# A softmax with relative position bias: the first loads are cut into pieces and spread over two DMA queues

## The chip, the cores and the metric

The kernel runs on one core of a Trainium2 chip. The core has engines that each run their own list of instructions: VectorE (DVE), ScalarE (ACT), GpSimd (POOL), SyncE (SP) and TensorE (PE, unused here). Data moves between the chip's memory (HBM) and the on-chip buffer (SBUF, 128 partitions) by DMA transfers, which an engine only issues; 16 DMA engines carry them out. The metric is the time of one execution in microseconds (us), the median of the runs; lower is better.

## The reference

Inputs are `logits` of shape 2 x 8 x 2112 x 2112 (float32) and a table `rel_bias` of 8 heads x 33 entries. For every head h, query i and key j the kernel adds a bias that depends on i - j alone, clipped to 16 on both sides, and takes the softmax over j:

```python
rel_clipped = np.clip(pos[:, None] - pos[None, :], -16, 16) + 16
logits = logits + rel_bias[:, rel_clipped][None]
exp = np.exp(logits - logits.max(axis=-1, keepdims=True))
return exp / exp.sum(axis=-1, keepdims=True)
```

Every element is read once and written once: 285.48 MB in and 285.48 MB out.

## The kernel before

**Tiling.** Partition p holds the rows of one head and one of 16 row regions, 132 rows of 2,112 elements for each of the two batches. A *chunk* is 6 such rows in every partition: 128 partitions x 12,672 elements, 6,336 KB, held by one of four buffers X0 to X3. A *window* is the four chunks m = 0 to 3 (two batches, two groups of six rows); 11 windows k = 0 to 10 make the whole, so there are 44 chunks. One partition's share of a chunk is one contiguous run of 50,688 B in HBM; in the texts below this run, which moves as one DMA packet, is called a **strip** (it holds six softmax rows).

**The order of work.** Everything is written by hand with semaphores; there is no scheduler.

- SP (lines 83 to 102): issues the four loads of window 0 at once (`load(0, m)`, line 99 calls line 91), then in a loop waits until the store of buffer m has landed (`take(nc.sync, st[m], 16)`) and issues the next window's load into that buffer. All loads of `logits` are on SP's queue (q1 in the profile).
- DVE: first a prologue (lines 120 to 169) that builds a table F of biases; then, per window, one copy of a part of it (`window`, line 172), and per chunk `add` (line 186, six instructions: add the bias, keep the negated row maximum), a reciprocal (line 210) and four of the six rescalings (line 213). `add(m)` begins with `take(v, ld[m], 16)`, that is: it waits until the chunk's load has landed.
- ACT: per chunk six exponentials (line 197), two rescalings (line 218), then it waits for all six rescaled rows and issues the store (line 95). All stores are on ACT's queue (q10), as is one small load of `rel_bias` in the prologue (line 122).

A transfer adds 1 to its semaphore for each DMA engine that is done with its share, by a packet of 4 B behind the share's data, called a **mark** below. 16 marks mean that the transfer has landed. One chunk's transfer is 128 strips and 16 marks: 8 strips and one mark for each DMA engine.

The waits in `take` (line 88) consume the count; the profile names line 88 where an engine was released by such a wait. The code of `add`, `window`, `load` and `store` and what calls them follows.

Of the kernel before, what the change touches and what calls it, by code (L numbers as in the profile page):

```python
# [15 lines left out]
def kernel(  # L16
# [6 lines left out]
    nc = tc.nc  # L23
    P = 128
    B, H, S, S2 = logits.shape
# [3 lines left out]
    RP = H * S // P  # L29
# [4 lines left out]
    NBUF = 4  # L34
    R = 6
    M = NBUF // B
    G = M * R
# [6 lines left out]
    X = [io.tile([P, R * S], FP32, tag=f"X{b}", name=f"X{b}") for b in range(NBUF)]  # L44
# [25 lines left out]
    def rows(t, k, m):  # L70
        return bass.AP(
            tensor=t.tensor, offset=t.offset + (m // M) * (H * S * S) + (m % M) * R * S + k * (G * S), ap=[[RP * S, P], [1, R * S]],
        )

    with tc.tile_critical(no_gpsimd_drain=True):  # L75
        ld = [nc.alloc_semaphore(f"ld{b}") for b in range(NBUF)]
        st = [nc.alloc_semaphore(f"st{b}") for b in range(NBUF)]
# [2 lines left out]
        scaled = nc.alloc_semaphore("scaled")  # L80
        inv = nc.alloc_semaphore("inv")
        rb = nc.alloc_semaphore("rb")
        zero = nc.alloc_semaphore("zero")
        idx = nc.alloc_semaphore("idx")
        dve = nc.alloc_semaphore("dve")

        def take(eng, sem, n):
            eng.wait_ge(sem, n).then_inc(sem, -n)  # L88

        def load(k, m):  # L90
            nc.sync.dma_start(out=X[m][:, :], in_=rows(logits, k, m)).then_inc(ld[m], 16)

        def store(k, m):
            take(nc.scalar, scaled, R)
            nc.scalar.dma_start(out=rows(out, k, m), in_=X[m][:, :]).then_inc(st[m], 16)

        for m in range(NBUF):
            load(0, m)
        with nc.Fori(0, K - 1, 1, engines=[ENG.SP]) as k:
            for m in range(NBUF):  # L100
                take(nc.sync, st[m], 16)
# [11 lines left out]
        def settle():  # L113
# [9 lines left out]
            out=bass.AP(tensor=F2.tensor, offset=F2.offset, ap=[[Q * step, P // Q], [1, H * W]]),  # L123
            in_=bass.AP(tensor=rel_bias.tensor, offset=rel_bias.offset, ap=[[0, P // Q], [1, H * W]]),
        ).then_inc(rb, 16)
        nc.gpsimd.iota(pid[:, :], pattern=[[0, 2]], base=0, channel_multiplier=1).then_inc(idx, 1)
        nc.gpsimd.iota(
            num, pattern=[[1, NB + 1]], base=0, channel_multiplier=0,
# [52 lines left out]

        def add(m):
            take(v, ld[m], 16)
            for i in range(R):
                x = G - 1 - (m % M) * R - i
                v.tensor_tensor_reduce(  # L186
                    out=row(m, i), in0=row(m, i), in1=F2[:, x : x + S],
                    scale=-1.0, scalar=BIG, op0=ALU.add, op1=ALU.min, accum_out=col(nmax, m, i),
                ).then_inc(added, 1)
# [25 lines left out]
        def scale_rest(m):  # L215
            scales_begin(nc.scalar, m)
            for i in range(DV, R):
                nc.scalar.activation(  # L218
                    out=row(m, i), in_=row(m, i), func=ACTF.Copy, scale=col(rec, m, i),
                ).then_inc(scaled, 1)  # L220

        with nc.Fori(0, K, 1, engines=[ENG.DVE]) as k:  # L222
            window(k)
            for m in range(NBUF):
                add(m)
                scale(m)
# [36 lines left out]
```

## Time and profile before

| what | value |
|---|---|
| time, median of 3 runs | 1325.94 us (1325.74 to 1336.57) |
| profiled execution, from its first to its last instruction (span) | 1323.8 us |
| DVE busy | 866.2 us, 65% of the span |
| ACT busy | 757.2 us, 57% |
| DMA | 570.98 MB, mean 431 GB/s |
| queue q1 (loads): packets, share of 16 DMA engines' span | 6336, 50.0% |
| queue q10 (stores and the bias table) | 6344, 49.8% |

The page gives no other time for the profiled execution than its span, which lies 2.1 us below the median of the runs.

How to read it: the page's busy shares of DVE and ACT are averages over the span. The DMA row cuts the span in 40 slices and gives the mean busy share of the 16 DMA engines in tenths; GB/s is what they moved in a slice. In a table of short stretches, a DMA packet counts where it begins, with its whole duration, so that a share can pass 1.00; the bytes divided by 50,688 then tell how many strips began there. A timeline row is start, duration, engine, line, operation, what it writes and reads, and in brackets how long the engine sat idle before it and what released it. An engine name with a q (SPq, ACTq, DVEq) is that engine's sequencer, which runs waits, branches and DMA issues.

### The profile page before, as it was taken

Reading aid. Unit: us, or ns where it says so; the run is one execution under the profiler, and the core shown is the slowest. Engines: PE = TensorE matmul, PEld = TensorE weight load, DVE = VectorE, ACT = ScalarE, POOL = GpSimd, SP = SyncE. Lnnn points to the kernel's source line nnn. Section 1 sums busy time; section 2 is a strip of 40 time slices with the busy share of each in tenths; the row PEclk is TensorE's granted clock in tenths of the full one; section 3 lists DMA queues with packets and bytes.
Section 4 is the critical chain, followed back from the end, with each engine's and each line's share of the span. In section 5 each row is a group of like instructions: output and inputs, shape, how many; then the busy total and the mean of one; then the engine's idle time right before and its main releaser. Section 6 shows DMA issues by size and latency. Waiting matters only on the chain. (4 is left out here: it accounts for less than half of the span.)

```text
span 1323.8 us, 2109 instructions
## 1 busy us (share of the span) xinstructions
DVE 866.2 (65%) x781; ACT 757.2 (57%) x627; POOL 0.4 (0%) x6
## 2 busy tenths in 40 slices
DVE  6886666566766675576667666556766576566662
ACT  3776655556666555555656555555666565555663
POOL 0000000000000000000000000000000000000000
DMA  9999999999999999999999999999999999999998
GB/s 417 417 423 435 441 435 423 441 438 421 440 441 427 430 441 435 424 440 438 424 437 440 437 423 440 440 421 438 441 432 426 441 437 423 440 440 423 437 441 369
DMA packets 12682, 570.98 MB, mean 431 GB/s; under 512 B 1412, under 2 KB 1416, under 8 KB 1416
## 3 DMA queue, kind: packets, MB, share of 16 engines
q1 hardware_dynamic: 6336, 285.48, 50.0%
q10 hardware_dynamic: 6344, 285.48, 49.8%
q14 instruction: 2, 0.02, 0.0%
HBM read 285.48 MB, written 285.47 MB: 431 GB/s over the span
## 5 line engine op out<-in xcount | busy, mean ns | idle before, releaser
L197 ACT ACTIVATE X<-X,nmax 128x2112 f32<-128x2112 f32 x264 | 542.6, 2055 | 505.1 <-DVE nmax L186 472.4
L186 DVE CUSTOM_DVE_ANT_0 X<-X,F 128x2112 f32<-128x2112 f32 x264 | 605.2, 2354 | 319.1 <-DVEq L88 319.1
L213 DVE TENSOR_SCALAR X<-X,rec 128x2112 f32<-128x2112 f32 x176 | 220.3, 1315 | 2.8
L218 ACT ACTIVATE X<-X,rec 128x2112 f32<-128x2112 f32 x88 | 176.1, 2048 | 17.2 <-DVE rec L210 12.2
L210 DVE RECIPROCAL rec<-tot 128x6 f32<-128x6 f32 x44 | 8.4, 191 | 106.2 <-DVEq L88 106.2
L197 ACT ACTIVATION_READ_ACCUMULATOR X<-X,nmax 128x1 f32 x264 | 49.2, 186 | 0.0
L197 ACT ACT_TABLE_LOAD x11 | 14.1, 1283 | 22.6 <-ACTq L88 19.9
L172 DVE COPY F<-F 128x2123 f32 x11 | 26.0, 2361 | 0.5 <-DVEq L88 0.5
L186 DVE DVE_READ_ACCUMULATOR2_ANT nmax<- 128x1 f32 x264 | 21.6, 82 | 0.0
L144 DVE LOAD_MASK_SELECT F<-F x1 | 0.0, 14 | 6.2 <-DMA F<-in_rel_bias_dram 6.2
L164 DVE COPY F<-own 128x1485 f32<-128x1485 f32 x1 | 1.7, 1698 | 0.0
L120 DVE MEMSET F<- 128x264 f32 x1 | 0.3, 278 | 1.1 <-SPq L75 1.1
L142 DVE TENSOR_SCALAR Z<-rec,Z 128x16 f32<-128x16 f32 (+2 forms) x5 | 0.8, 233 | 0.1
L163 DVE TENSOR_TENSOR F<-F,own 128x528 f32<-128x528 f32 x1 | 0.7, 717 | 0.1
L160 DVE TENSOR_TENSOR F<-Z,own 128x528 f32<-128x528 f32 x1 | 0.7, 705 | 0.0
L150 DVE TENSOR_REDUCE own<-F 128x33 f32<-128x264 f32 x1 | 0.6, 609 | 0.1
L147 DVE TENSOR_TENSOR F<-F,Z 128x264 f32<-128x264 f32 x1 | 0.4, 429 | 0.1
L144 DVE STREAM_SHUFFLE F<-F 128x264 f32<-128x264 f32 x1 | 0.4, 442 | 0.0
L158 DVE SCALAR_TENSOR_TENSOR own<-Z,own 128x16 f32<-128x16 f32 x1 | 0.2, 235 | 0.2 <-DVEq L88 0.2
L155 DVE TENSOR_SCALAR own<-Z,own 128x16 f32<-128x16 f32 x1 | 0.2, 235 | 0.2 <-DVEq L88 0.2
L166 DVE COPY F<-own 128x115 f32<-128x115 f32 x1 | 0.3, 271 | 0.0
L168 DVE COPY F<-own 128x115 f32<-128x115 f32 x1 | 0.3, 271 | 0.0
(11 smaller groups left out, 1.6 us busy)
## 6 DMA issues: line engine op xcount, KB each, us to landing
X<-in_logits_dram SPq DMA_DIRECT2D x44, 6336.0 KB, 38.4
out_dram<-X ACTq DMA_DIRECT2D x44, 6336.0 KB, 59.0
F<-in_rel_bias_dram ACTq DMA_DIRECT2D x1, 4.1 KB
```

The source lines that it names most:

```text
L142: then(v.tensor_scalar(out=o, in0=num[:, 0:n], scalar1=s, scalar2=None, op0=op))
L144: then(v.stream_shuffle(out=T, in_=T, mask=[0] * Q))
L150: then(v.tensor_reduce(out=rbK, in_=view(F2, H * W, [[1, W], [W, H]]), axis=mybir.AxisListType.X, op=ALU.add))
L160: then(v.tensor_tensor(out=bands, in0=view(eq, 0, [[1, NB], [0, W]]), in1=view(rbK, W - 1, [[0, NB], [-1, W]]), op=ALU.mult))
L163: then(v.tensor_tensor(out=bands, in0=bands, in1=view(rest, 0, [[1, NB], [0, W]]), op=ALU.add))
L164: then(v.tensor_copy(out=view(F, C0 + W, [[RP, NB - 1], [1, RP - W]]), in_=view(reg, 1, [[1, NB - 1], [0, RP - W]])))
L172: then(v.tensor_copy(out=F2[:, 0:SW], in_=F[:, bass.ds(RP - G - k * G, SW)]))
L186: v.tensor_tensor_reduce(out=row(m, i), in0=row(m, i), in1=F2[:, x : x + S], scale=-1.0, scalar=BIG, op0=ALU.add, op1=ALU.min, accum_out=c ...
L197: nc.scalar.activation(out=row(m, i), in_=row(m, i), func=ACTF.Exp, scale=-1.0, bias=col(nmax, m, i), accum_out=col(tot, m, i),).then_inc( ...
L210: v.reciprocal(out=col(rec, m, 0, R), in_=col(tot, m, 0, R)).then_inc(inv, 1 if m < NBUF - 1 else NBUF + 1)
L213: v.tensor_scalar_mul(out=row(m, i), in0=row(m, i), scalar1=col(rec, m, i)).then_inc(scaled, 1)
L218: nc.scalar.activation(out=row(m, i), in_=row(m, i), func=ACTF.Copy, scale=col(rec, m, i),).then_inc(scaled, 1)
```

## The change

The first loads of the four buffers are issued in another form; the loop that issues all later loads and all stores is as before.

- X0's first load is cut into two halves of three rows each: the first half on SP's queue, the second on ACT's, with a semaphore of its own (`head0`). DVE waits for `head0` once, ahead of its loop.
- X1's first load is cut into its last row (SP, semaphore `head1`) and the five rows before it (ACT).
- X2's first load is as before.
- X3's first load is cut into five rows of all partitions, the last row of partitions 0 to 119, and the last row of partitions 120 to 127, all on SP; the two transfers of the last row count on `head3`.
- `add(1)` and `add(3)` wait for these semaphores too. In later windows `head1` and `head3` are already past the awaited count.
- ACT issues its two loads behind that of `rel_bias`.

On SP's list of instructions, at the start of the program (X_58 to X_61 are the buffers X0 to X3; the shape is partitions x elements), stood before:

```order
L91 DMA X_58<-in_logits_dram 128x12672
L91 DMA X_59<-in_logits_dram 128x12672
L91 DMA X_60<-in_logits_dram 128x12672
L91 DMA X_61<-in_logits_dram 128x12672
L99 UNCONDITIONAL_BRANCH
```

and stands now:

```order
L103 DMA X_58<-in_logits_dram 128x6336
L103 DMA X_59<-in_logits_dram 128x2112
L100 DMA X_60<-in_logits_dram 128x12672
L103 DMA X_61<-in_logits_dram 128x10560
L103 DMA X_61<-in_logits_dram 120x2112
L103 DMA X_61<-in_logits_dram 8x2112
L117 UNCONDITIONAL_BRANCH
```

Four transfers have become six on this queue, three of them for X3. On ACT's list, also at the start, stands now:

```order
L140 DMA F2_62<-in_rel_bias_dram 4x264
L103 DMA X0_58<-in_logits_dram 128x6336
L103 DMA X1_59<-in_logits_dram 128x10560
L97 UNCONDITIONAL_BRANCH
L252 UNCONDITIONAL_BRANCH
L221 ACT_TABLE_LOAD
L221 ACTIVATE X0_58,tot_66<-X0_58,nmax_65 128x2112 x6
```

The two rows at L103 are new; they stand ahead of ACT's loop. On DVE's list, at the entry of its loop (in brackets the semaphores awaited), stands now:

```order
L247 UNCONDITIONAL_BRANCH [waits dve,head0]
L247 ISA
L192 ISA
L192 COPY F_62<-F 128x2123
L210 ISA X_58,nmax<-X_58,F_62 128x2112 [waits dve,ld0]
```

The wait for `head0` is in the first of these rows, ahead of the window's copy (L192); before, that row waited for `dve` alone and the only wait for X0's load stood behind the copy. The diff:

```diff
--- before.py
+++ after.py
@@ -72,6 +72,12 @@
             tensor=t.tensor, offset=t.offset + (m // M) * (H * S * S) + (m % M) * R * S + k * (G * S), ap=[[RP * S, P], [1, R * S]],
         )
 
+    def part(t, k, m, a, b, p=0, n=P):
+        return bass.AP(
+            tensor=t.tensor, offset=t.offset + (m // M) * (H * S * S) + ((m % M) * R + a) * S + k * (G * S) + p * RP * S,
+            ap=[[RP * S, n], [1, (b - a) * S]],
+        )
+
     with tc.tile_critical(no_gpsimd_drain=True):
         ld = [nc.alloc_semaphore(f"ld{b}") for b in range(NBUF)]
         st = [nc.alloc_semaphore(f"st{b}") for b in range(NBUF)]
@@ -80,6 +86,9 @@
         scaled = nc.alloc_semaphore("scaled")
         inv = nc.alloc_semaphore("inv")
         rb = nc.alloc_semaphore("rb")
+        head0 = nc.alloc_semaphore("head0")
+        head1 = nc.alloc_semaphore("head1")
+        head3 = nc.alloc_semaphore("head3")
         zero = nc.alloc_semaphore("zero")
         idx = nc.alloc_semaphore("idx")
         dve = nc.alloc_semaphore("dve")
@@ -90,12 +99,21 @@
         def load(k, m):
             nc.sync.dma_start(out=X[m][:, :], in_=rows(logits, k, m)).then_inc(ld[m], 16)
 
+        def load_part(eng, m, a, b, sem, p=0, n=P):
+            eng.dma_start(out=X[m][p : p + n, a * S : b * S], in_=part(logits, 0, m, a, b, p, n)).then_inc(sem, 16)
+
         def store(k, m):
             take(nc.scalar, scaled, R)
             nc.scalar.dma_start(out=rows(out, k, m), in_=X[m][:, :]).then_inc(st[m], 16)
 
-        for m in range(NBUF):
-            load(0, m)
+        HALF = R // 2
+        load_part(nc.sync, 0, 0, HALF, ld[0])
+        load_part(nc.sync, 1, R - 1, R, head1)
+        load(0, 2)
+        UP = P - P // 16
+        load_part(nc.sync, NBUF - 1, 0, R - 1, ld[NBUF - 1])
+        load_part(nc.sync, NBUF - 1, R - 1, R, head3, 0, UP)
+        load_part(nc.sync, NBUF - 1, R - 1, R, head3, UP, P - UP)
         with nc.Fori(0, K - 1, 1, engines=[ENG.SP]) as k:
             for m in range(NBUF):
                 take(nc.sync, st[m], 16)
@@ -123,6 +141,8 @@
             out=bass.AP(tensor=F2.tensor, offset=F2.offset, ap=[[Q * step, P // Q], [1, H * W]]),
             in_=bass.AP(tensor=rel_bias.tensor, offset=rel_bias.offset, ap=[[0, P // Q], [1, H * W]]),
         ).then_inc(rb, 16)
+        load_part(nc.scalar, 0, HALF, R, head0)
+        load_part(nc.scalar, 1, 0, R - 1, ld[1])
         nc.gpsimd.iota(pid[:, :], pattern=[[0, 2]], base=0, channel_multiplier=1).then_inc(idx, 1)
         nc.gpsimd.iota(
             num, pattern=[[1, NB + 1]], base=0, channel_multiplier=0,
@@ -181,6 +201,10 @@
 
         def add(m):
             take(v, ld[m], 16)
+            if m == 1:
+                v.wait_ge(head1, 16)
+            if m == NBUF - 1:
+                v.wait_ge(head3, 32)
             for i in range(R):
                 x = G - 1 - (m % M) * R - i
                 v.tensor_tensor_reduce(
@@ -219,6 +243,7 @@
                     out=row(m, i), in_=row(m, i), func=ACTF.Copy, scale=col(rec, m, i),
                 ).then_inc(scaled, 1)
 
+        v.wait_ge(head0, 16)
         with nc.Fori(0, K, 1, engines=[ENG.DVE]) as k:
             window(k)
             for m in range(NBUF):
```

## The prediction

> **What bounds the kernel now.** The page first: the DMA engines, not the compute engines, are full.
>
> ```profile
> span 1323.8 us, 2109 instructions
> DMA  9999999999999999999999999999999999999998
> DMA packets 12682, 570.98 MB, mean 431 GB/s; under 512 B 1412, under 2 KB 1416, under 8 KB 1416
> q1 hardware_dynamic: 6336, 285.48, 50.0%
> q10 hardware_dynamic: 6344, 285.48, 49.8%
> ```
>
> The two queues' shares add up to 99.8% of the span: no slice has spare DMA time to fill, and the bytes stay the same. A change can then gain only at the two ends, and lose wherever it leaves the DMA engines without work. The small stretches at both ends show how little there is:
>
> ```profile
> 4.00:5.00 1.00, 0.00 (x0) 0.00 (x0) 0.00 (x0) 1.00 1.75 760
> 1305.00:1318.00 13.00, 0.00 (x0) 0.00 (x0) 0.00 (x0) 1.00 0.98 425
> 1319.00:1320.00 1.00, 0.00 (x0) 0.00 (x0) 0.00 (x0) 1.00 0.01 0
> 1320.00:1320.50 0.50, 0.00 (x0) 0.00 (x0) 0.00 (x0) 1.00 0.24 101
> 1320.50:1323.80 3.30, 0.00 (x0) 0.00 (x0) 0.00 (x0) 1.00 0.00 0
> ```
>
> 760 GB/s for 1 us is 15 strips; the share of 1.75 on 16 engines makes 1.87 us for each. The engines are full to 1318 (0.98). In the last stretches no strip begins from 1319 to 1320, and then a single one (101 GB/s x 0.5 us = 50.7 KB): one DMA engine is a strip later than the fifteen others. That engine's lag, about 1.9 us, is all that a better balance could win at the end.
>
> What the end hangs on is in the timeline and in the time from a transfer's issue to its landing:
>
> ```profile
> 1281.59 2.36 DVE L186 CUSTOM_DVE_ANT_0 X<-X,F 128x2112 f32<-128x2112 f32 x1 [8.54 <-DVEq L88]
> 1303.34 0.34 ACTq L95 DMA_DIRECT2D out_dram<-X  x1
> DMA to landing us min/median/max: 19.3/19.3/19.3
> ...
> DMA to landing us min/median/max: 17.6/17.6/17.6
> ```
>
> The last chunk's load lets DVE go at 1281.59; its store is issued 21.75 us later, at 1303.34, and lands 19.3 us after that (first landing row), at 1322.6; 1.2 us later the span ends. The second landing row is the very first load, alone on idle engines: 17.6 us. So the last store waits 2 to 3 us for others to drain, and no more: **after the last load there is just enough store backlog to cover 22 us of computing.** If loads ran later against stores than now, the DMA engines would stand idle there.
>
> **How the two queues share.** That is the question the change turns on. Four stretches of 1.87 us in a row, then a longer one, of the DMA queues (packets, MB, share):
>
> ```profile
> q10 hardware_dynamic: 12, 0.61, 75.1%
> q1 hardware_dynamic: 4, 0.20, 25.0%
> ...
> q1 hardware_dynamic: 12, 0.61, 75.1%
> q10 hardware_dynamic: 4, 0.20, 25.0%
> ...
> q10 hardware_dynamic: 188, 8.72, 53.0%
> q1 hardware_dynamic: 189, 7.96, 48.4%
> ```
>
> From 56.00 twelve engines move a store strip and four a load strip, and from 57.87 the reverse (59.74 and 61.61 repeat it): each engine takes one packet of a queue, then one of the other. The longer stretch, 47 to 85 us, tells what is shared equally: 188 packets against 189, but 8.72 MB against 7.96. The loads had 32 marks among their packets, the stores 16, and a mark of 4 B cost the loads a whole turn. So **turns are equal, not bytes**: a small packet on SP's queue lets a whole store strip of 1.87 us pass for it.
>
> The Trainium skill (DMA: Bandwidth & Descriptors, Queues, rings and completion order) agrees that the engine goes round between queues by packet, but says that a packet drains some 9 to 17 descriptors before it switches. The rows above show one strip for each turn; whether strips of 8,448 B would go several to a turn, no row here shows. By that sentence X3's eight small strips could pass in one turn; what that would make of the time is the first rival below.
>
> **The change part by part.** Sizes first, from 1.87 us by bytes: a half chunk's piece (25,344 B) 0.94 us, five rows (42,240 B) 1.56, one row (8,448 B) 0.31. These are estimates; smaller pieces could cost more. The 47-to-85 rows bound a packet's own overhead: 8.72 MB in 53.0% and 7.96 in 48.4% are the same share for each MB, with twice the marks, so I take none, and at most 0.5 us in all for some 25 more packets on an engine.
>
> *X0 in two halves.* Both queues use the same 16 engines, so nothing lands sooner by it. X0 needs 15.0 us for its eight strips' worth; the first packets are some 0.6 us slow and begin at 2.0 (the first load's 17.6 holds both). SP's half ends first; then X1's last row on SP takes turns with ACT's half, some five of 0.31. X0 is complete at 2.0 + 0.6 + 15.0 + 1.6 = 19.2 instead of 18.6.
>
> ```profile
> 15.79 2.37 DVE L172 COPY F<-F 128x2123 f32 x1 [0.50 <-DVEq L88]
> 18.71 2.36 DVE L186 CUSTOM_DVE_ANT_0 X<-X,F 128x2112 f32<-128x2112 f32 x1 [0.56 <-DVEq L88]
> 40.38 0.38 ACTq L95 DMA_DIRECT2D out_dram<-X  x1
> ```
>
> And the copy of the window, until now done at 15.79 while the load was under way, stands behind the wait for `head0`: the first add comes at 19.2 + 2.4 + 0.6 = 22.2, 3.5 us late, the first store at 43.9. Behind the waiting instruction stands the whole loop of DVE, and ACT's exponentials wait for it. All of window 0 on DVE shifts by 3.5 as long as loads are there. DMA loses nothing: with no store yet, three chunks (24 strips, 44.9 us) run until 47.5, and X3 is still queued. Bounds: 0 to 4 us later.
>
> *X1 in two pieces.* X1's five rows on ACT's queue alternate with the rest of the last row (four turns of 1.87) and then with X2's strips (four of 3.43): complete at 19.2 + 7.5 + 13.7 = 40.4 instead of 33. DVE asks for it at 22.2 + 21.3 = 43.5, so 3 us of cover are left; without them each microsecond would delay the second store, itself queued behind the first until 76. X2 follows at 47.9. Cost: nothing.
>
> *X3 in three pieces.* This is the term that counts. From about 48 on, stores take turns with SP's queue.
>
> ```profile
> 85.36 2.36 DVE L186 CUSTOM_DVE_ANT_0 X<-X,F 128x2112 f32<-128x2112 f32 x1 [2.58 <-DVEq L88]
> 107.14 0.34 ACTq L95 DMA_DIRECT2D out_dram<-X  x1
> 83.35 0.34 ACTq L95 DMA_DIRECT2D out_dram<-X  x1
> ```
>
> Before, X3 has nine turns (8 strips, 1 mark), so about nine store strips pass with it, and DVE gets it at 85.36. Now an engine has for it 8 pieces of five rows, a mark, 8 of one row, a mark, and on the engines that carry the 8-partition piece one more and a mark: 20 turns. (The table of 4 partitions put 4 packets and 4 marks on q10: 6344 against 6336. So small transfers are spread one to an engine; I take 8 engines for this one.) Two of the turns between are marks of the first two stores, so about 18 store strips pass instead of 9. The load bytes are the same, so X3 comes 9 x 1.87 = 17 us later, at 102. DVE would have been ready at 82.8 + 3.5. The fourth store is issued at 107.14 + 17 = 124.
>
> Part of this is given back at once. The third store, issued at 83.35 + 3.5, has about six strips left at 102 and alternates until 102 + 6 x 3.74 = 124; then the store queue is empty until the fourth arrives at 125 to 126, and one or two load strips run alone. That leaves 13; engines without the last small piece are two turns (3.7 us) ahead. Between 10 and 13 I take **11.5 us** by which loads lag from window 1 on. Does it heal later? Each queue then has work waiting at all times:
>
> ```profile
> X<-in_logits_dram SPq DMA_DIRECT2D x44, 6336.0 KB, 38.4
> out_dram<-X ACTq DMA_DIRECT2D x44, 6336.0 KB, 59.0
> ```
>
> A transfer that alternates needs 30 us (16 turns of 1.87). A store lands after 59, so it waits 29 in its queue; 11.5 less leaves 17. Loads wait 8, and will wait longer. Equal turns keep the lag through all ten later windows, at no cost, until the end.
>
> *The end.* Last load 1281.59 + 11.5 = 1293.1; last store issued 21.75 later, 1314.8. The earlier stores were done by about 1305 before, and the same work is done by then now, so the engines idle for some 10 us. The store alone lands in 17.6 less the 1 us of a slow first strip, 16.6: 1331.4; the span ends at 1332.6, **8.8 us above 1323.8**. The late engine's 1.9 us is inside the wait and neither gains nor costs. The bounds of the lag, 8.5 to 14.5 (another 1.5 either way on the count of turns), give 1329.6 to 1335.6.
>
> *The rest at nothing.* SP's two more issues and ACT's two (0.34 each) lie ahead of ACT's first exponential at 21; DVE's two more waits are passed in later windows.
>
> By the same page (How many engines, and the table of measured facts) a transfer of 120 partitions runs on 15 engines, one of 8 on 8, always the lowest-numbered, and engines 7 and 15 tend to be slow. The sixteenth would then be spared eight small strips, 8 x 0.31 = 2.5 us, about the late engine's lag; which engine is late, the rows do not say.
>
> **The rivals.**
>
> 1. *Small strips share a turn*, or shares go by bytes. Then X3 costs two or three extra turns (marks), 4 to 6 us of lag, less the first store's coming 3.5 later; the 2 to 3 us of slack at the end cover it. Time within 2 us of before in the span, 1325 to 1328 measured. Against it: one strip for each turn, and a turn for 4 B.
> 2. *The other side: the balance wins.* The same, and the late engine is the one that the 120-partition piece spares. The lone strip at 1320.0 goes; eight engines carry 0.31 more. Span 1323.8 - 1.9 + 0.3 = 1322.2. It decides only if the lag stays under the slack of 2 to 3 us; above that, the end hangs on the last load.
> 3. *Over 1% slower: the 8-partition piece falls on one engine* that has its full share already. That engine has seven more small strips, 7 x 1.87 = 13 us more lag, and each landing waits for it: 8.8 + 13 = 22 us, 1348. The one-to-an-engine count of the 4-partition table speaks against it.
>
> **How the numbers follow.** The sum is made against the profiled 1323.8; the median, 1325.94, is 2.1 above, and I add that: 1332.6 + 2.1 = **1334.7**. Chances: forecast 0.74 (1331 to 1338), first rival 0.12, second 0.07 (1323.8 to 1325), third 0.07. The range 1326.5 to 1339 leaves out the second and third rival, part of the first and a tail of the forecast, 2 in 10. 1% is 13 us, about what a measurement of this kernel can tell from no change: faster 0.01, within 0.92, slower 0.07; the forecast, 0.7%, lies inside.
>
> **What would show it.** Right: first add at 22, X3's add near 102 instead of 85.36, the last add near 1293, and a stretch of some 10 us around 1310 with hardly a DMA packet. Wrong: X3's add near 86 to 90 with eight or more small strips begun in one turn; a slow engine that still ends alone; or X3 late but the last add at 1282, which would mean that later windows heal the lag.

## The result and the profile after

The changed kernel takes **1513.17 us** (median of 6, 1509.12 to 1521.77); the kernel before, on the same chip, 1325.97 (median of 6). The ratio is 1.1415 with a 95% interval from 1.1381 to 1.1448: 14% slower, where 0.7% was forecast. The ratios below leave out executions more than 1.5% above the fastest of the same kernel, and none is given where half of the executions or more would be left out. The page of the profiled execution after (11 rows; the last two are transfers: number, size of each, median us from issue to landing):

```profile
span 1509.3 us, 2113 instructions
DVE 866.3 (57%) x781; ACT 757.2 (50%) x627; POOL 0.4 (0%) x6
GB/s 409 387 405 403 392 390 399 395 384 388 383 386 372 388 376 387 369 384 372 387 380 384 371 390 383 372 384 382 386 382 373 371 384 384 386 367 388 388 292 230
DMA packets 13121, 570.98 MB, mean 378 GB/s; under 512 B 1467, under 2 KB 1471, under 8 KB 1471
...
q10 hardware_dynamic: 6632, 294.13, 47.6%
q1 hardware_dynamic: 6487, 276.83, 46.8%
...
out_dram<-X ACTq DMA_DIRECT2D x44, 6336.0 KB, 46.4
X<-in_logits_dram SPq DMA_DIRECT2D x41, 6336.0 KB, 67.7
```

The compute engines do the same work (DVE 866.3 us against 866.2). The bytes are the same. What changed is the rate, and not at the two ends: it is low in the second slice already (387 GB/s), and about 380 through all later windows, although the lines that issue the loads and stores of those windows are word for word the old ones. The edit touches three of the 88 large transfers and slows all of them.

The transfers' times say how. Chunk for chunk, a buffer goes through one circle: load issued to landed, 21.75 us of computing, store issued to landed, and some 0.4 us until the next load of that buffer is issued. With four buffers one circle is four chunks. Before: 38.4 + 59.0 + 22.2 = 119.6, a fourth of which is 29.9 us for a chunk. After: 67.7 + 46.4 + 22.2 = 136.3, 34.1 us. The difference of 4.2 us times 44 chunks is 185 us, and the span grew by 1509.3 - 1323.8 = 185.5. **So the whole loss is a slower pace in every window**; no single window carries it. The timeline shows the pace: DVE's first adds of chunks, those that waited for a load.

```profile
22.98 2.36 DVE L210 CUSTOM_DVE_ANT_0 X<-X,F 128x2112 f32<-128x2112 f32 x1 [0.31 <-DVEq L97]
44.64 0.38 ACTq L107 DMA_DIRECT2D out_dram<-X  x1
100.96 2.36 DVE L210 CUSTOM_DVE_ANT_0 X<-X,F 128x2112 f32<-128x2112 f32 x1 [13.92 <-DMA X<-in_logits_dram]
122.73 0.34 ACTq L107 DMA_DIRECT2D out_dram<-X  x1
134.40 2.36 DVE L210 CUSTOM_DVE_ANT_0 X<-X,F 128x2112 f32<-128x2112 f32 x1 [9.63 <-DVEq L97]
169.55 2.36 DVE L210 CUSTOM_DVE_ANT_0 X<-X,F 128x2112 f32<-128x2112 f32 x1 [13.74 <-DVEq L97]
205.42 2.36 DVE L210 CUSTOM_DVE_ANT_0 X<-X,F 128x2112 f32<-128x2112 f32 x1 [14.45 <-DVEq L97]
```

The rows are X0's first add, the first store, X3's add, the fourth store, and then the first three chunks of window 1 (X0, X1, X2). From 134.40 on a chunk takes 35 to 36 us. The same three adds before:

```profile
115.27 2.36 DVE L186 CUSTOM_DVE_ANT_0 X<-X,F 128x2112 f32<-128x2112 f32 x1 [6.10 <-DVEq L88]
145.18 2.36 DVE L186 CUSTOM_DVE_ANT_0 X<-X,F 128x2112 f32<-128x2112 f32 x1 [8.49 <-DVEq L88]
175.08 2.36 DVE L186 CUSTOM_DVE_ANT_0 X<-X,F 128x2112 f32<-128x2112 f32 x1 [8.49 <-DVEq L88]
```

What the DMA engines do meanwhile, from 900 to 1200 us, far from both ends. The kernel before:

```profile
q10 hardware_dynamic: 1441, 64.93, 50.0%
q1 hardware_dynamic: 1440, 64.88, 50.0%
```

The changed kernel, the same stretch; its GB/s row gives 7.5 us a value (the kernel before has 433 in 39 of its 40, and 439 in one):

```profile
GB/s 392 318 426 372 365 419 338 419 338 419 358 406 358 392 426 270 426 399 399 345 426 351 406 406 304 392 419 338 365 399 419 324 426 284 406 426 385 358 365 399
...
q1 hardware_dynamic: 1258, 56.47, 47.9%
q10 hardware_dynamic: 1267, 57.38, 46.9%
```

Two things, both to be worked out from these rows. The shares add up to 94.8% instead of 100%: engines are idle for 5% of the time. And a strip takes longer: 47.9% of 16 x 300 us for 56.47 MB, which is 1,114 strips, makes 2.06 us each for loads, in the same way 1.99 for stores, against 1.87 before. 2.03 / 1.87 is 8%, and 1.08 / 0.948 is 1.14: the loss. The uneven GB/s values (270 to 426) fit two queues that no longer interleave steadily.

Why engines can be idle although transfers wait, the marks tell. A buffer is let go by the last of a load's 16 marks, and the trace has the time of each. The time from the first mark of a transfer to its last is called its **spread** below. In the kernel before, the spread of every load from window 1 on is 2.6 us; in the changed kernel the median is 47.9 us. Two rows of q1 show it, the kernel before from 1278 to 1282 us (its last load) and the changed kernel from 911 to 913 (a load of X0):

```profile
q1 hardware_dynamic: 16, 0.00, 0.2%
...
q1 hardware_dynamic: 13, 0.20, 27.3%
```

The first row is all 16 marks. The second is four strips (0.20 MB) and nine marks: nine engines are done with X0, and the marks of the other seven follow from 953 to 959 us. **The 16 DMA engines have come out of step**, and those ahead wait for those behind; e1 below shows it engine by engine.

### The profile page after: what moved, and what is told of

It reads as the page before. It is cut to its first block, busy times and chain, and to the rows that moved or that the text cites. A ratio compares the mean times of both kernels' runs of the same rounds, so it can differ in the third digit from the quotient of the medians.

```text
span 1509.3 us, 2113 instructions
## 1 busy us (share of the span) xinstructions
DVE 866.3 (57%) x781; ACT 757.2 (50%) x627; POOL 0.4 (0%) x6
## 2 busy tenths in 40 slices
DMA packets 13121, 570.98 MB, mean 378 GB/s; under 512 B 1467, under 2 KB 1471, under 8 KB 1471
## 3 DMA queue, kind: packets, MB, share of 16 engines
q1 hardware_dynamic: 6487, 276.83, 46.8%
## 5 line engine op out<-in xcount | busy, mean ns | idle before, releaser
L237 DVE TENSOR_SCALAR X<-X,rec 128x2112 f32<-128x2112 f32 x176 | 220.3, 1315 | 2.8
L192 DVE COPY F<-F 128x2123 f32 x11 | 26.0, 2364 | 6.0 <-DMA X<-in_logits_dram 6.0
## 6 DMA issues: line engine op xcount, KB each, us to landing
out_dram<-X ACTq DMA_DIRECT2D x44, 6336.0 KB, 46.4
X<-in_logits_dram SPq DMA_DIRECT2D x41, 6336.0 KB, 67.7
```

The source lines that it names most:

```text
L192: then(v.tensor_copy(out=F2[:, 0:SW], in_=F[:, bass.ds(RP - G - k * G, SW)]))
L237: v.tensor_scalar_mul(out=row(m, i), in0=row(m, i), scalar1=col(rec, m, i)).then_inc(scaled, 1)
```

## The experiments

No kernel here leaves out part of the computation; those with extra loads read 8 KB more for each, into a buffer that nothing uses. Of each edit the lines that issue transfers are shown; the waits that go with them are left out, and so is, where the start is the kernel before, the loop over `load(0, m)` that they replace. A lag below is that of window 1's first add against 115.27. Letters in the expectations stand for the theories of the moment: A for DMA engines with unequal shares; D, and later F, for loads that fall so far behind the stores that the stores' queue has too little left waiting in it. All results in one table; the two columns of waits are the median us from issue to landing of the whole-chunk loads and of the stores, and the last column is the median spread of the loads from window 1 on, worked out from the marks in the traces.

| kernel | median us (number) | ratio, 95% interval | loads | stores | sum | spread |
|---|---|---|---|---|---|---|
| before | 1325.97 (6) | | 38.4 | 59.0 | 97.4 | 2.6 |
| the change | 1513.17 (6) | 1.1415 [1.1381, 1.1448] | 67.7 | 46.4 | 114.1 | 47.9 |
| e1_112_16 | 1499.29 (4) | | 67.9 | 46.6 | 114.5 | 48.6 |
| e2_x3_only | 1335.34 (10) | 1.0056 [1.0035, 1.0078] | 50.7 | 46.7 | 97.4 | 9.8 |
| e3_x01_only | 1332.31 (10) | 1.0038 [1.0009, 1.0067] | 40.1 | 57.5 | 97.6 | 3.8 |
| e4_whole_120_8 | 1345.86 (4) | 1.0132 [1.0087, 1.0176] | 44.0 | 53.5 | 97.5 | 16.5 |
| e5_tiny4 | 1492.62 (4) | 1.1181 [1.1113, 1.1249] | 68.0 | 46.5 | 114.5 | 47.9 |
| e5_tiny8 | 1340.17 (4) | 1.0048 [1.0000, 1.0097] | 41.7 | 57.6 | 99.3 | 9.1 |
| e6_x0_x3 | 1341.08 (4) | 1.0068 [1.0026, 1.0111] | 50.9 | 46.6 | 97.5 | 12.3 |
| e7_bal_x0 | 1329.79 (6) | 0.9997 [0.9963, 1.0032] | 40.5 | 57.1 | 97.6 | 7.0 |
| e8_tiny2 | 1333.78 (10) | 1.0035 [1.0001, 1.0068] | 55.3 | 42.1 | 97.4 | 4.0 |
| e8_tiny3 | 1526.33 (4) | 1.1481 [1.1421, 1.1541] | 69.2 | 47.8 | 117.0 | 48.0 |
| e9_order | 1332.85 (10) | 1.0029 [1.0002, 1.0056] | 48.5 | 49.4 | 97.9 | 10.3 |
| e10_after_tiny6 | 1513.53 (4) | | 67.7 | 46.5 | 114.2 | 48.0 |
| f1_one_queue | 1419.05 (4), in two groups | | 46.4 | 51.6 | 98.0 | 12.7 |
| f2_x1_x3 | 1342.63 (10) | 1.0100 [1.0075, 1.0124] | 51.9 | 44.7 | 96.6 | 11.0 |
| f3_row_whole | 1540.63 (4) | 1.1543 [1.1467, 1.1619] | 69.9 | 48.6 | 118.5 | 48.3 |

Read the last two columns first: there are **two kinds of runs and nothing between**. In one the waits add up to 97 to 99 us, however they are divided between loads and stores, and the median spread is under 17 us; in the other they add up to 114 to 119, the spread is 48, and the kernel loses 12 to 15%. (Waits and spread are those of the profiled execution, the times those of all. An execution that changes over late lies between in time.)

### Is it one edit, or unequal shares of the DMA engines?

**e1_112_16**: the change, with X3's last row cut at partition 112 instead of 120, which gives all 16 engines the same bytes.

```diff
-        UP = P - P // 16
+        UP = P - P // 8
```

> The changed kernel with one number altered: X3's last row goes as transfers of 112 and 16 partitions instead of 120 and 8, so that each of the 16 DMA engines can get the same number of pieces (7 and 1). All pieces, queues and waits stay. Theory A (unequal shares put the DMA engines out of step, and that is what slows all later windows): the 190 us are gone, 1330 to 1340 us, because only the lag of the loads that the prediction worked out is left. Theory B (loads that run later against stores, or small pieces between store strips, bring loads and stores into a slow pattern): 1490 to 1515 us, as the changed kernel.

Measured: executions of 1501.84, 1531.32, 1496.73 and 1367.37. The packet counts bear out how the pieces were dealt out: q1 has 6,496 packets against the change's 6,487, which is 32 marks for the two transfers of the last row instead of 23. So 120 partitions ran on 15 engines and 8 on 8, while 112 and 16 ran on 16 each. (The Trainium skill, DMA: Bandwidth & Descriptors, How many engines, gives the same: the largest number up to 16 that divides the partitions. This trace agrees, 15 + 8 = 23.) Equal shares did not help: unequal shares are not the cause, and theory A falls. But the run is instructive in another way; its GB/s row, 37.5 us a value:

```profile
GB/s 411 385 411 434 433 431 427 424 427 405 376 389 389 349 389 384 373 388 378 378 388 383 376 368 369 389 388 389 368 387 389 370 388 369 369 368 389 388 227 181
```

Here the full rate held to about 340 us. The pace was lost earlier: the adds of window 1 stand at 131.91, 161.85 and 191.71, at the old pace, and the next two at 226.54 and 262.07. From there the loads' spread grows with every chunk, from 4.0 us (the load landed at 192) to 49 (at 402). While it grows the engines ahead still have transfers to move, so the rate hides the loss. That is a state that tips over, not a cost that something pays each window. The one execution of 1367.37 must have lost far less; there is no trace of it.

Once the spread has stopped growing, e1 can be read engine by engine. Queue q1 from 625 to 628 us, the same from 659.7 to 662.4 (q10 has no packet there), and the next store's issue:

```profile
q1 hardware_dynamic: 16, 0.05, 4.2%
...
q1 hardware_dynamic: 1, 0.05, 4.3%
...
661.64 0.34 ACTq L107 DMA_DIRECT2D out_dram<-X  x1
```

The first row is one strip and fifteen marks of a load of X0; the sixteenth mark comes at 674. In the second row one strip begins in 2.7 us: fifteen engines have nothing to do until the store is issued at 661.64, and its chunk had itself been let go by the last engine's mark at 639.7. Fourteen rounds between 537 and 1358 us, each from one load mark of the last engine to its next, can be followed packet by packet. In each the last engine moves its 16 strips without a pause, 2.14 us each or 34.3 for a chunk: **in e1 the pace is that of one DMA engine, and the other fifteen wait for it.** Its strips take 1.87 us (median) while the fifteen move the other way, and 2.49 while they move the same way; why, no run shows.

**e2_x3_only** and **e3_x01_only**: the two halves of the change apart. In e2 X0 and X1 are loaded whole and X3 in three pieces; in e3 X0 and X1 are in parts on both queues and X3 is whole.

```diff
 e2, against the kernel before
+        load(0, 0)
+        load(0, 1)
+        load(0, 2)
+        UP = P - P // 16
+        load_part(nc.sync, NBUF - 1, 0, R - 1, ld[NBUF - 1])
+        load_part(nc.sync, NBUF - 1, R - 1, R, head3, 0, UP)
+        load_part(nc.sync, NBUF - 1, R - 1, R, head3, UP, P - UP)
 e3, against the change
-        load_part(nc.sync, NBUF - 1, 0, R - 1, ld[NBUF - 1])
-        load_part(nc.sync, NBUF - 1, R - 1, R, head3, 0, UP)
-        load_part(nc.sync, NBUF - 1, R - 1, R, head3, UP, P - UP)
+        load(0, NBUF - 1)
```

> The kernel before with X3's first load alone in the changed form (five rows, then the last row over 120 and 8 partitions); X0 and X1 are loaded whole by SP. Theory A (unequal shares): 1480 to 1515 us. Theory C (the two queues carrying loads at the start are to blame): 1326 to 1336 us.

> The changed kernel with X3's first load whole again; X0 and X1 stay in parts on both queues. Theory A: 1324 to 1332 us, since every DMA engine has equal shares and the loads lag little. Theory C (two queues): 1480 to 1515 us.

Measured: 9.3 and 6.3 us over their kernel before (1326.02), where both together cost 187. The halves do not add up. **e2 is the forecast's mechanism without the rest**, and it can be read against the forecast. Its timeline (X3's add, the first three chunks of window 1, the last add, the last store), and its windows before the end (busy time of DVE and ACT, then clock, DMA share, GB/s):

```profile
104.42 2.36 DVE L203 CUSTOM_DVE_ANT_0 X<-X,F 128x2112 f32<-128x2112 f32 x1 [21.64 <-DMA X<-in_logits_dram]
128.54 2.36 DVE L203 CUSTOM_DVE_ANT_0 X<-X,F 128x2112 f32<-128x2112 f32 x1 [0.30 <-DVEq L95]
152.08 2.36 DVE L203 CUSTOM_DVE_ANT_0 X<-X,F 128x2112 f32<-128x2112 f32 x1 [2.11 <-DVEq L95]
181.97 2.36 DVE L203 CUSTOM_DVE_ANT_0 X<-X,F 128x2112 f32<-128x2112 f32 x1 [8.47 <-DVEq L95]
...
1293.26 2.36 DVE L203 CUSTOM_DVE_ANT_0 X<-X,F 128x2112 f32<-128x2112 f32 x1 [8.59 <-DVEq L95]
1315.01 0.34 ACTq L105 DMA_DIRECT2D out_dram<-X  x1
...
1305.00:1310.00 5.00, 2.44 (x4) 4.33 (x5) 0.00 (x0) 1.00 0.10 41
1310.00:1315.00 5.00, 4.78 (x4) 3.75 (x2) 0.00 (x0) 1.00 0.00 0
```

The idle stretch around 1310, the last add at 1293 and the last store at 1315 are where the forecast had them. The way there is not: the lag is 13.3 us at window 1's first chunk, but 6.9 at the next two, and it grows again by 4.8 us over the 37 chunks from 181.97 to 1293.26, which take 30.03 us each against 29.90. Where half of the lag went, the DMA queues of e2 show in two stretches of 2 us, from 122 and from 124:

```profile
q1 hardware_dynamic: 18, 0.86, 99.5%
...
q1 hardware_dynamic: 32, 0.91, 105.7%
q10 hardware_dynamic: 1, 0.05, 5.8%
```

One engine began one store strip in these 4 us, the others none: the loads had nearly all engines to themselves and caught up.

### Lag alone, without the change's pieces

**e4_whole_120_8**: the kernel before, with X3's whole strips sent as 120 + 8 partitions, which spreads the marks over time but adds two turns on eight engines, where the change adds eleven. **e5_tiny4**, **e5_tiny8** and, in a later round, **e8_tiny2** and **e8_tiny3**: the kernel before, with 4, 8, 2 or 3 extra loads of 8 KB behind the first four loads on SP's queue.

```diff
 e4
+        load_part(nc.sync, NBUF - 1, 0, R, ld[NBUF - 1], 0, UP)
+        load_part(nc.sync, NBUF - 1, 0, R, head3, UP, P - UP)
 e5 and e8, with n extra loads
+        for n in range(4):
+            nc.sync.dma_start(
+                out=scr[16 * (n % 8) : 16 * (n % 8) + 16, 0:128],
+                in_=bass.AP(tensor=logits.tensor, offset=logits.offset + n * 128, ap=[[RP * S, 16], [1, 128]]),
+            ).then_inc(extra, 16)
```

> The kernel before with X3's first load as two transfers of whole six-row strips over 120 and 8 partitions: no small pieces, 17 marks or turns fewer than in the changed kernel, but one engine has no strip of it and eight have nine. Theory A: 1480 to 1515 us, as the difference between engines is eight to nine strips again. Theory B (small pieces and lag): 1324 to 1332 us.

> The kernel before, with four extra loads of 16 partitions x 512 B on SP's queue behind the first four loads (32 KB in all, into a buffer that nobody reads). Each gives every DMA engine one packet and one mark, two turns, so that two store strips pass: loads lag by 4 x 2 x 1.87 = 15 us from window 1 on. All chunks are loaded whole by one queue. Theory D (there is a limit to the lag: as long as stores wait in their queue, the lag costs only its idle time at the end; when the stores' time from issue to landing has shrunk to the 30 us of 16 turns, the queue runs dry and the loop falls into the slow pattern): below the limit, loads land after 53 us, stores after 44 to 45, time 1336 to 1341 us. Theory E (the lag is harmless, the parts over two queues bring the DMA engines out of order): also 1336 to 1341 us.

> The same with eight extra loads of 16 partitions x 512 B: 30 us of lag, which uses up the stores' wait of 59 - 30 = 29 us. Theory D: the limit is reached, 1450 to 1520 us, and the two queues' shares of DMA time add up to less than 96%. Theory E: every chunk is loaded whole and by one queue, so the loop stays at its pace of 29.9 us for each chunk and only idles up to 20 us at the end: 1340 to 1348 us.

Measured: e4 keeps its pace and pays 20 us once (its GB/s row begins 410 376 297 395 and then stands at 434), so marks that come far apart do not by themselves start the slow regime: its spread is 16.5 us for loads and 26.5 for stores all through, and it does not grow. e5_tiny4 falls into it: **32 KB in four small loads, 0.006% of the bytes, cost 12%**, with every chunk whole, all loads on one queue and nothing of the change's pieces. q1 has 128 packets more than before, 4 x (16 strips + 16 marks): two turns an engine for each extra load, eight for the four. The first three chunks of window 1 in e5_tiny4:

```profile
128.55 2.36 DVE L194 CUSTOM_DVE_ANT_0 X<-X,F 128x2112 f32<-128x2112 f32 x1 [19.77 <-DVEq L90]
156.61 2.36 DVE L194 CUSTOM_DVE_ANT_0 X<-X,F 128x2112 f32<-128x2112 f32 x1 [6.64 <-DVEq L90]
188.99 2.36 DVE L194 CUSTOM_DVE_ANT_0 X<-X,F 128x2112 f32<-128x2112 f32 x1 [10.96 <-DVEq L90]
```

The first is where e2 has it (128.54), and from there they part. e2 had met its empty store queue at 122 and caught up; e5_tiny4 meets it at 150, since its fourth store, issued on time at 106.74, had drained by then and the next was issued at 150.21. Its queues from 150, 154 and 158, in stretches of 2 us:

```profile
q1 hardware_dynamic: 20, 1.01, 117.0%
q10 hardware_dynamic: 9, 0.00, 0.3%
...
q10 hardware_dynamic: 17, 0.86, 101.1%
q1 hardware_dynamic: 9, 0.00, 0.3%
...
q10 hardware_dynamic: 16, 0.81, 100.7%
```

First loads alone, then stores alone: now the loads' queue runs empty as well, because no store had landed to free a buffer. The two queues have stopped alternating and take the engines in blocks.

e5_tiny8 should have been worse by the lag theory and was not: 1375.57, 1343.02, 1333.13 and 1337.33. Its first load of window 1 came 30 us late (add at 145.56), the store queue was empty for longer, loads ran alone until they had made up all but some 9 us (the fourth add of window 1 is at 213.73, before at 204.97), and the loop went on with stores at 57.6. So "more lag, more loss" is wrong. What counts is what the loop settles into after the queue has run dry. The profiled execution is the longest of the four, and it lost its pace after all, but only past 1030 us. Three adds there, then the transfers' waits from 800 to 1100 us:

```profile
1031.58 2.36 DVE L194 CUSTOM_DVE_ANT_0 X<-X,F 128x2112 f32<-128x2112 f32 x1 [8.62 <-DVEq L90]
1063.70 2.36 DVE L194 CUSTOM_DVE_ANT_0 X<-X,F 128x2112 f32<-128x2112 f32 x1 [10.71 <-DVEq L90]
1097.85 2.36 DVE L194 CUSTOM_DVE_ANT_0 X<-X,F 128x2112 f32<-128x2112 f32 x1 [10.35 <-DVEq L90]
...
X<-in_logits_dram SPq DMA_DIRECT2D x10, 6336.0 KB, 40.4
out_dram<-X ACTq DMA_DIRECT2D x10, 6336.0 KB, 58.3
```

The chunks take 32 and 34 us from there on, though stores had the same reserve as in the kernel before (58.3 us to land) until then. That speaks against a theory by the reserve alone: a loop with the full reserve can tip as well. What did change in between is the spread: that of the stores grew from 2.6 us (the store landed at 202) to 23 (at 931) while the pace held, and after 1031 that of the loads grew from 7 us to 47. So 58.3 us is the wait for the last engine; the first was done with a store some 23 us sooner.

> The kernel before with two extra loads of 16 partitions x 512 B behind the first four loads: four more turns for SP's queue on each DMA engine. Theory F (loads come later by what stores get ahead, so the stores' time in the queue shrinks by both, 7.5 us for each extra load; above some 10 us of rest beyond the 30 us of 16 turns the loop is steady, near zero it falls apart): stores land after about 44 us, loads after about 54, steady pace of 29.9 us for each chunk, 1328 to 1335 us. Theory G (any disturbance of the order of turns can start the slow pattern, whatever rest is left): 1450 to 1520 us.

> The same with three: theory F: the stores' rest is 59 - 22 - 30 = 6 to 7 us, at the edge; 1400 to 1520 us, or 1332 to 1340 if 6 us are still enough. Theory G: 1450 to 1520 us.

Measured: two extra loads settle, three do not, and the step from 1333.78 to 1526.33 is one load of 8 KB. The first chunks of window 1 with two extra loads, then with three:

```profile
122.61 2.36 DVE L194 CUSTOM_DVE_ANT_0 X<-X,F 128x2112 f32<-128x2112 f32 x1 [13.70 <-DVEq L90]
152.59 2.36 DVE L194 CUSTOM_DVE_ANT_0 X<-X,F 128x2112 f32<-128x2112 f32 x1 [8.56 <-DVEq L90]
```

```profile
130.53 2.36 DVE L194 CUSTOM_DVE_ANT_0 X<-X,F 128x2112 f32<-128x2112 f32 x1 [20.99 <-DVEq L90]
165.91 2.36 DVE L194 CUSTOM_DVE_ANT_0 X<-X,F 128x2112 f32<-128x2112 f32 x1 [13.96 <-DVEq L90]
```

e8_tiny2 prices a turn cleanly: four turns of 1.87 us are 7.5, and the lag is 122.61 - 115.27 = 7.3. (The Trainium skill, DMA: Bandwidth & Descriptors, Queues, rings and completion order, has a packet drain some 9 to 17 descriptors before the engine goes to the other queue. By this run a strip of 512 B and a mark of 4 B each cost a turn of their own.) It also prices what a lag does to the stores: they land in 42.1 instead of 59.0, 16.9 us earlier, about **twice** the lag, while loads land 16.9 us later. That is what a fixed sum means: the DMA engines are full, so a microsecond that loads lose is one that stores win, and a store is then both issued later by it and drained earlier.

### The pieces again: pairs, order, queues

**e6_x0_x3** and **f2_x1_x3**: the change with X1 whole, and with X0 whole.

```diff
 e6
-        load_part(nc.sync, 1, R - 1, R, head1)
-        load_part(nc.scalar, 1, 0, R - 1, ld[1])
+        load(0, 1)
 f2
-        load_part(nc.sync, 0, 0, HALF, ld[0])
-        load_part(nc.scalar, 0, HALF, R, head0)
+        load(0, 0)
```

> The changed kernel with X1's first load whole on SP's queue again; X0 in halves on both queues, X3 in its three pieces. Theory D: X3's pieces give the lag of some 11 us and the late start of stores adds a little, so loads land after 50 to 60 us and the loop is below the limit: 1334 to 1345 us; if the lag reaches the limit here too, 1450 to 1520. Theory E: two queues carry parts, so 1450 to 1520 us.

> The changed kernel with X0's first load whole on SP's queue; X1 in two parts on both queues and X3 in its three pieces. X1's five rows now take turns with X0, so the first add comes some 10 us later and so do the stores, while loads go on. Theory F: a later start of the stores gives loads a lead, so the stores keep more rest: 1335 to 1350 us. If X1's part on ACT's queue together with X3's pieces is harmful in itself: 1490 to 1520 us.

Measured: 11.1 and 15.8 us over their kernels before (1329.99 and 1326.88), both at the full pace. So each pair of the three edits costs 0.4 to 1.0% and keeps the pace; only all three reach the slow regime.

**e7_bal_x0**: the kernel before, with X0's last row (and no other) in 120 + 8 partitions, first in SP's queue, where no store is waiting. It tests the second rival, the spared engine, without any lag.

```diff
+        load_part(nc.sync, 0, 0, R - 1, ld[0])
+        load_part(nc.sync, 0, R - 1, R, head0, 0, UP)
+        load_part(nc.sync, 0, R - 1, R, head0, UP, P - UP)
```

> The kernel before with the uneven piece moved to where no store is under way: X0's first load goes as five rows, then the last row over 120 and 8 partitions, all on SP; X1, X2 and X3 whole. Small pieces cost no store a turn there, so no lag. If the 120-partition piece spares the engine that ends 1.9 us late: 1324 to 1325.5 us; if another engine is late, or the early piece changes nothing at the end: 1325.5 to 1327 us. If any unequal share is harmful in itself: above 1331 us.

Measured: 1329.79 against 1329.99. Nothing is won by the balance, within 0.3%.

**e9_order**: exactly the change's transfers, with X3's last-row pieces issued ahead of X2, where they take turns with ACT's two loads and not with stores.

```diff
-        load(0, 2)
         UP = P - P // 16
-        load_part(nc.sync, NBUF - 1, 0, R - 1, ld[NBUF - 1])
         load_part(nc.sync, NBUF - 1, R - 1, R, head3, 0, UP)
         load_part(nc.sync, NBUF - 1, R - 1, R, head3, UP, P - UP)
+        load(0, 2)
+        load_part(nc.sync, NBUF - 1, 0, R - 1, ld[NBUF - 1])
```

> The changed kernel with the same transfers on the same queues, in another order on SP: the two small transfers of X3's last row are issued ahead of X2's load and X3's five rows behind it, so the small pieces take their turns while no store is under way. Theory F: X3 no longer costs extra turns against stores, so stores keep their rest, as with X0 and X1 in parts alone: 1328 to 1340 us. Theory H (pieces on two queues together with uneven shares disorder the DMA engines for good): 1480 to 1520 us.

Measured: 1332.85, the full pace, loads 48.5 and stores 49.4. **The same transfers, with the same 13,121 packets, in another order, cost 0.3% instead of 14%.** So neither the number of pieces nor the use of both queues is enough; what e9 takes away is that X3's smallest packets pass while stores take turns with them. That alone is not enough either: in e2 they do, and it keeps its pace.

**e10_after_tiny6**: the change plus six extra loads, to push it over into the recovery of e5_tiny8.

> The changed kernel with six extra loads of 16 partitions x 512 B on SP's queue behind X3's pieces: 22 us more lag for window 1's first load, so even more work at a disadvantage. Theory F: the stores run dry for all DMA engines at once for a long time, the loads catch up alone, and the loop goes on with a full rest: faster than the changed kernel in spite of the added transfers, 1335 to 1390 us. Theory H: not faster than the changed kernel, 1500 to 1530 us.

Measured: 1513.53, no recovery. Its adds of window 1 stand at 136.46, 160.75 and 195.48: the second came 24 us after the first, the catching up that was hoped for, and the third 35 after that. But the first add came 2 us later than in the changed kernel (134.40), not 22, so the added lag hardly arose, and whether a larger one would have healed the loop is not tested.

**f1_one_queue** and **f3_row_whole**: the change with all parts of X0 and X1 on SP's queue; and the change with X3's last row as one transfer of 128 partitions, which takes two turns away.

```diff
 f1
-        load_part(nc.scalar, 0, HALF, R, head0)
-        load_part(nc.scalar, 1, 0, R - 1, ld[1])
+        load_part(nc.sync, 0, HALF, R, head0)
+        load_part(nc.sync, 1, 0, R - 1, ld[1])
 f3
-        load_part(nc.sync, NBUF - 1, R - 1, R, head3, 0, UP)
-        load_part(nc.sync, NBUF - 1, R - 1, R, head3, UP, P - UP)
+        load_part(nc.sync, NBUF - 1, R - 1, R, head3)
```

> The changed kernel with all its pieces, but X0's and X1's parts on SP's queue alone, in the order first half, second half, last row, five rows. Theory F (what counts is the rest of the stores in their queue; X3's pieces take 12 us of it, and the two queues at the start take the remainder): X3's pieces alone stay below the limit, loads land after 48 to 55 us, 1332 to 1345 us. Theory J (that X0, X1 and X3 come in pieces is enough, on whatever queue): 1490 to 1520 us.

> The changed kernel with X3's last row as one transfer over 128 partitions: 18 turns for X3 on each DMA engine instead of 20, and equal shares. Theory F: two turns give back 4 to 7 us of rest; if the changed kernel is past the limit by less than that, 1333 to 1400 us, if by more, 1490 to 1520 us as with 112 and 16 partitions (19 turns), which fell into the slow pattern 200 us later than the changed kernel.

Measured: f1 took 1337.15, 1336.87, 1502.53 and 1500.95 us in four executions of one program. Such a kernel has no time to be quoted: it stands at the edge, and which way it goes is decided by less than the program fixes. f3 took 1540.63, no better than the change, so the 120/8 cut in itself is not what does the harm, and the change is not past the edge by just its two turns.

## Why the prediction was wrong

**The step that failed** is the one at the end of X3's part: "A store lands after 59, so it waits 29 in its queue; 11.5 less leaves 17 ... Equal turns keep the lag through all ten later windows, at no cost, until the end." Instead each chunk took 34.1 us for 29.9, 185 us in all. Two things are wrong in the step.

First, the size. It took the lag off the stores' wait once. With a fixed sum it comes off about twice: e8_tiny2 lost 16.9 us for a lag of 7.3, e2 lost 12.3 for one that settled at 6.9. (It is no law: e5_tiny8, some 9 us late, kept 57.6.) For 11.5 us that leaves, by an estimate from these two, not 17 of the 29 us but about 29 - 2 x 11.5 = 6. The lag itself was larger, too: window 1's first add is at 134.40, 19.1 us late.

Second, "at no cost" assumed that a store queue costs nothing until it is empty, that being empty costs idle time once, and that the 16 DMA engines stay together. The runs show a second regime that keeps itself going: the engines come apart, to a spread of 48 us, and each transfer waits for its last engine (in e1 one engine sets the pace for all). Steady kernels in the table have stores at 42.1 us or more, that is 12 us beyond the 30 us of 16 turns. Below that, runs differ: e2's fourth store lands after 36.1 us, and e2 recovers; e5_tiny4's next store lands after 38.8, and it does not; e1 kept its pace for three chunks of window 1 and then lost it; f1 went both ways. e5_tiny8 tipped past 1030 us with stores at 58. So a thin reserve fits most of the slow runs (between two and three extra loads in the kernel before lies an edge), but it is not a condition. The spread tells which regime a run is in; what makes it grow in one run and stand still in e4 is not shown.

Point by point:

- *What bounds the kernel*: right. The DMA engines were full, and the loss is their idle 5% and their 8% longer strips. The prediction looked for loss only where engines would have no work, and never asked whether 1.87 us for a strip would stay.
- *Equal turns*: right, and the most useful reading. The price of a turn (7.3 us measured for 7.5) confirms it, and the 15 + 8 marks the eight engines that were taken for the last piece.
- *X0*: the first add 22.98 for 22.2, the first store 44.64 for 43.9: right. "DMA loses nothing" was wrong: with X0 and X1 alone in parts (e3) the first three slices moved 402, 403 and 398 GB/s against 417, 417 and 423, some 54 GB/s over 33 us or 1.8 MB, 4 us of work at 434. e3's first add of window 1 is at 121.82, 6.6 late, and its span 1329.6, 5.8 longer. There everything shifts together, and the stores keep their wait (57.5): a late start is not a lag of loads against stores, and it is harmless to the pace.
- *X1*: "cost: nothing" holds for X1's own add, but X1's parts take their share in the slow start and, with X0's and X3's, in the loss. 
- *X3*: X3's add 100.96 for 102, the fourth store 122.73 for 124: right in place. In the changed kernel the strips were slow by then: in 2 us from 50 and from 57, 16 store strips began, with these shares of 16 engines:

```profile
q10 hardware_dynamic: 16, 0.81, 93.6%
...
q10 hardware_dynamic: 16, 0.81, 118.3%
```

  93.6% of 2 us is 1.87 us for a strip, 118.3% is 2.37. In both stretches all 16 engines start a store strip together, where before twelve and four were on different queues; that alone does not make a strip slow, as the first row shows.
- *The end*: right where the pace held. In e2 the idle 10 us before the last store and the place of the last add came out as forecast, and with them 1335.34 us for 1334.7. That agreement is partly luck: half of the lag was made up in window 1, and 0.13 us a chunk was lost later.
- *Rivals*: the first (small strips share a turn) falls by X3's add and by e8_tiny2. The second gets no support: e7's interval of 0.3% either way is wider than the 1.6 us at stake, but its trace still ends with single late strips (51 GB/s from 1324 to 1325 us, and again to 1326); which engine is late, no trace names. The third put the price on the right side for the wrong reason: the 8-partition piece ran on eight engines (eight marks), not one. The case that came, a change of pace in all windows, was not among them, and the range to 1339 had no room for it.

**Open.** The last engine of e1 accounts for that run's pace, but why its strips take longer while the other engines move the same way is not shown, nor is the changed kernel, with nine engines ahead and seven behind, followed as closely. What makes the first engine fall behind is not settled. An empty store queue fits e5_tiny4 and the start of e5_tiny8 as quoted, but e5_tiny8 tipped late with stores at 58 us, and in the changed kernel strips are slow from 57 us, some 7 us after the first store's strips began. What the runs settle is smaller: a start-up in which small packets take turns with stores starts it (e9 against the change, e8_tiny2 against e8_tiny3), by turns and not by bytes or unequal shares. And why any two of the three edits are steady while the three are not is known from the runs, not explained.

## What to carry to other kernels

Where loads and stores share full DMA engines through a ring of few buffers, add up issue-to-landing of loads, computing and issue-to-landing of stores: it must be buffers times pace, and at a fixed pace what one side loses in its queue the other wins; in two runs a lag of 7 us cost the stores' reserve about twice that. Small packets are dear wherever the other queue has large ones waiting, since each, even a mark of 4 B, lets a large one pass; put them where that queue is empty, as e9 did. Judge a start-up edit by the pace of the later windows and by several executions, since the loop can tip into a slower regime that none of these traces leaves. Look at the first and the last mark of a transfer, and not only at its landing: a median can look healthy while the DMA engines come apart.

## What the runs showed that was not expected

- The loop has two stable paces for one program: 29.9 us a chunk with full DMA engines (434 GB/s), and 34 to 35 with about 380 GB/s, idle 5% and 2.0 us instead of 1.87 for a strip of 50,688 B. f1 was found in both, e1 left the first after its load of 192 us and e5_tiny8 past 1030. None of these traces shows a way back.
- 24 KB more in three small loads cost 200 us (e8_tiny3), 16 KB in two cost 6, and 64 KB in eight some 10.
- A lag that empties the store queue can heal, since loads then run alone (e2 in part, e5_tiny8 for all but some 9 us, and not for good).
- In the slow regime the 16 marks of one load lie 48 us apart instead of 2.6. In e1 a single engine is behind, and fifteen wait for it in every chunk.
